# Layer 0's value and gate projections of a two-layer encoder: seven products of halves by Strassen's scheme in place of eight

## The chip, the cores and the metric

The kernel runs on one core of a Trainium2 chip. The metric is the time of one execution on the device, in microseconds (us). Engines are named as in the profile: PE is TensorE (PEld are its weight loads), DVE is VectorE, ACT is ScalarE, POOL is GpSimd, SP is SyncE, which starts most of the transfers.

## The reference

The input is x of 512 tokens by 1024 features. There are two layers, each with a normalisation that is modulated by a condition c, a mixer, and a gated residual. Layer 0's mixer is retention with 4 heads, layer 1's is forgetting attention. What matters here is the input of layer 0:

```python
shift, scale, gate = jnp.split(c_act @ mod_w[i] + mod_b[i], 3, axis=-1)
h = _rms_norm(x, norm_g[i]) * (1.0 + scale[:, None, :]) + shift[:, None, :]
...
q, k, v, g = jnp.split(h @ w_in, [RET_DK, 2 * RET_DK, 2 * RET_DK + RET_DV], axis=-1)
```

For each of the 4 heads, q and k have 256 columns of `w_in`, v and g have 512. So v and g of a head are two products of h (512 x 1024) with 1024 x 512 weights, eight such products in all. q and k get a rotation by position. v is later used with its mean over the 512 columns of a head taken off, g goes through SiLU. All is float32.

## The kernel before

Every float32 product is made of three matmuls in the type fp32r: an operand is split into a head (ACT casts it to fp32r: `wh` for weights, the first `act` for activations) and a rest (what is left, by a subtraction on DVE or, in a few places, on POOL: `wl` and the second `act`). The function `mm3` adds head x head, head x rest and rest x head in a PSUM bank.

The weights come in as blocks of 512 KB ([128, 1024] words, tile `raw`), in one list that sets their order (class `Stream`). The class `WItem` loads a block and splits it. Blocks of `mod_w` (class `MItem`) stream between them; their steps (tile `macc`, one operation of 512 words for 128 rows) make the modulation for layer 0 at the start, and later, spread over the heads of layer 0, gate of layer 0 and modulation of layer 1.

The start: x is normalised and transposed. `make_h` makes, for each of 8 groups of 128 features, the modulated activations h, transposed ([128 features, 512 tokens]), with ACT once as head and once in full, and the rest on DVE. As these come, q and k of head 0 and q of head 1 are projected in six PSUM banks (tile `s`). POOL and DVE make the table of cosine and sine (tiles `tg`, `trig`). Then `rope` rotates: four DVE products of 512 words per projection (`rt`), and two additions and two rests on POOL (`rt`, `act`).

Then come heads 0 to 3 (`head`): q and k by `proj_qk`, where the weights stand and h moves; v and g by `proj_b`, where a block of h stands (128 features by 128 tokens) and 512 columns of weights move: 4 token tiles x 8 feature blocks x 3 = 96 matmuls of 512 columns per projection, into four banks of kind `p`. `evac_v` copies a bank with its sum and makes head and rest of v less its mean, `evac_g` puts SiLU of a bank in the tile `big`. Beside the projections of head h runs the retention of head h - 1 (`merge` gives it 0.45 of the projections' TensorE time). After it come the output projection of layer 0 (tile `a`), the second normalisation, and layer 1.

The order of instructions on each engine is not the program's. The class `Sched` collects all instructions as tasks, plays them through a simple model of the engines, with a price for each (`cost`), a number of buffers for each kind of tile (`KINDS`) and a priority from the program's place, and emits them in the order in which that model starts them. So a changed price or pool moves instructions everywhere. Each engine then takes its instructions strictly in that order. All instructions have one line in the profile, that of the emitting call (L430), so groups are told apart by their tiles.

Of the kernel before, what the change touches and what calls it, by code (L numbers as in the profile page):

```python
# [43 lines left out]
KINDS = {  # L44
# [3 lines left out]
    "goh": ("C", 16), "wo": ("C", 16), "raw": ("B", N_B), "wh": ("W", 3), "wl": ("W", 3),  # L48
# [11 lines left out]
def host_constants():  # L60
# [6 lines left out]
    # sums over the tokens up to c: [m, c] for the diagonal block, ones after it  # L67
# [10 lines left out]
class View:  # L78
    """A part of a buffer that may have no address yet: slices are taken once the buffer has one.
    `part` and `idx` say which partitions and words it covers."""  # L80
# [21 lines left out]
    def rearrange(self, pattern, **sizes):  # L102
        """Of "p (a b) -> p a b" and "p a b -> p (a b)", the only forms in use."""
# [35 lines left out]
class Buf:  # L139
# [6 lines left out]
    def touch(self, task, view, write):  # L146
        """The earlier tasks that an access has to follow."""
# [20 lines left out]
class Sched:  # L168
    """Collects the instructions of the kernel with what they read and write, plays them through a
    simple model of the core (engines in order of their own, transfers, memory slots) and emits  # L170
# [61 lines left out]
    def cost(self, t, op, args, kw, ins, outs):  # L232
# [8 lines left out]
        if t.eng == "PE":  # L241
            if op == "transpose":
                t.cols = 256
                return 0.107
# [265 lines left out]
def trunk(tc, x, c, positions, mod_w, mod_b, norm_g, ret_w_in, ret_w_out, fox_w_in, fox_b_f,  # L510
# [6 lines left out]
    with ExitStack() as es:  # L517
# [280 lines left out]
        def W(key, i=0):  # L798
            it = st.need(where[key] + i)
            return it.h, it.l  # L800
# [693 lines left out]
```

## Time and profile before

| | before |
|---|---|
| time, median of 3 runs | 757.44 us (756.97 to 757.86) |
| span of the profiled execution | 757.8 us (the page gives no other time for it; the runs' times lie within 0.9 us of it) |
| granted TensorE clock, mean | 0.989 |
| bytes moved | 105.73 MB, mean 140 GB/s |
| instructions | 10002 |

How to read it: times are counted from the span's start. A group of instructions has its engine, operation, tiles (out<-in), shapes and number, and behind the bar the time in which one of them was busy, the mean duration of one in ns, and the idle time of the engine just before them with what ended it. For PE the moving operand stands first among the inputs, then the stationary one, so `p<-wh,act` is a matmul that moves weights past standing activations. A timeline's row has start and length of a run of like instructions. [...]

### The profile page before, as it was taken

What the parts mean: (1) busy time and instruction counts of PE and PEld (TensorE: products, weight loads), DVE (VectorE), ACT (ScalarE), POOL (GpSimd) and SP (SyncE); (2) the same over time, 40 slices, a digit from 0 to 9 for tenths busy, and PEclk for the clock granted to TensorE, in tenths of its full rate; (3) what the DMA queues carried; (4) which work ended last, traced back from release to release, by engine and by line L of the source; (5) the groups of instructions that cost most, each with busy time, mean ns of one, the idle gap of its engine ahead of it and who ended that gap; (6) DMA issues with size and microseconds to landing.
All of it is one profiled execution on the core that took longest, in us unless ns stands there. A gap on an engine that the chain in (4) does not pass through costs nothing.

```text
span 757.8 us, 10002 instructions
## 1 busy us (share of the span) xinstructions
PE 735.2 (97%) x3478; PEld 603.2 (80%) x3478; DVE 540.3 (71%) x1168; ACT 359.5 (47%) x688; POOL 160.6 (21%) x156
## 2 busy tenths in 40 slices
PE   8999999999999999999999999999999899999995
PEld 6777888888888888888888887678888788888884
DVE  5886745865585458757764477978798879889945
ACT  7433623244224332443323255438576567777723
POOL 3437800300330033000000100342133422221011
PEclk9899999999999999999999999999999999999999
DMA  8993251644255334504532513434334425658002
GB/s 285 349 328 122 64 195 56 192 156 140 83 167 161 131 112 132 187 30 131 175 116 96 219 56 128 150 135 108 117 96 135 133 53 133 160 137 301 0 1 111
DMA packets 69730, 105.73 MB, mean 140 GB/s; under 512 B 6200, under 2 KB 35120, under 8 KB 69680
## 3 DMA queue, kind: packets, MB, share of 16 engines
q1 hardware_dynamic: 66320, 98.78, 40.4%
q0 software_dynamic: 3360, 6.32, 3.5%
q8 instruction: 27, 0.44, 0.2%
q14 instruction: 23, 0.19, 0.1%
HBM read 96.64 MB, written 4.25 MB: 133 GB/s over the span
## 4 chain that ended last, share of the span: by engine, by line
PE 79%; DVE 7%; issue 1%; ACT 1%; DMA 1%; POOL 1%; SPq 0%; POOLq 0%; ACTq 0%; DVEq 0%
PE p L430 46%; PE a L430 17%; PE r L430 15%; DVE t L430 3%; DVE wl L430 1%; DVE lg L430 1%; DVE macc L430 1%; POOL qn L430 1%; DMA ck<-cum_dram 1%; ACT tm L430 0%; DVE z L430 0%; DVE ph L430 0%; ACT qn L430 0%; DMA cum_dram<-tm 0%; DVE x L430 0%
## 5 line engine op out<-in xcount | busy, mean ns | idle before, releaser
L430 DVE TENSOR_TENSOR wl<-raw,wh 128x1024 fp32r<-128x1024 f32 x92 | 119.2, 1296 | 81.7 <-ACT wh L430 76.1
L430 ACT CAST wh<-raw 128x1024 fp32r<-128x1024 f32 x96 | 100.4, 1049 | 155.9 <-PE p L430 94.3
L430 PE MATMUL p<-wh,act 128*128 128x512 f32 x512 | 161.3, 391 | 1.8 <-DVE rt L430 1.8
L430 PE MATMUL p<-wh,big 128*128 128x512 f32 x384 | 134.8, 404 | 0.0
L430 PEld LDWEIGHTS p<-wh,act 128*128 128x128 f32 x512 | 96.0, 188 | 22.0 <-DVE rt L430 2.2
L430 PE MATMUL p<-wl,act 128*128 128x512 f32 x256 | 99.8, 390 | 0.0
L430 PEld LDWEIGHTS p<-wh,big 128*128 128x128 f32 x384 | 71.9, 189 | 14.8
L430 DVE SCALAR_TENSOR_TENSOR macc<-raw,csilu,macc 128x512 f32<-128x512 f32 x82 | 77.2, 941 | 1.2
L430 PE MATMUL p<-wl,big 128*128 128x512 f32 x192 | 76.6, 399 | 0.0
L430 PE MATMUL a<-wh,act 128*128 128x512 f32 x192 | 62.4, 398 | 0.6 <-ACT act L430 0.6
L430 POOL TENSOR_TENSOR rt<-rt,rt 128x512 f32<-128x512 f32 x16 | 25.3, 1599 | 176.4 <-DVE rt L430 176.4
L430 PEld LDWEIGHTS p<-wl,act 128*128 128x128 f32 x256 | 48.1, 188 | 9.9
L430 PE MATMUL p<-act,wh 128*128 128x512 f32 x160 | 53.8, 394 | 0.0
L430 POOL TENSOR_TENSOR ck<-ck,mask 128x256 f32<-128x256 f32 x32 | 28.1, 898 | 118.3 <-DMA ck<-cum_dram 81.9
L430 PE MATMUL p<-big,wh 128*128 128x512 f32 x128 | 44.4, 411 | 0.0
L430 ACT ACTIVATE lg<-lg,t 128x128 f32<-128x128 f32 (+1 forms) x64 | 36.1, 565 | 15.9 <-DVE t L430 15.2
L430 PEld LDWEIGHTS a<-wh,act 128*128 128x128 f32 x192 | 36.0, 188 | 8.2 <-ACT act L430 0.8
L430 PEld LDWEIGHTS p<-wl,big 128*128 128x128 f32 x192 | 36.4, 189 | 5.9
L430 PE MATMUL r<-act,sh 128*128 128x512 f32 x120 | 40.0, 394 | 0.0
L430 PE MATMUL a<-wl,act 128*128 128x512 f32 x96 | 37.8, 394 | 0.0
L430 POOL DMA_DIRECT2D x_dram<-x x8 | 4.4, 552 | 144.1 <-DVE x L430 137.6
L430 PEld LDWEIGHTS p<-act,wh 128*128 128x128 f32 x160 | 30.0, 188 | 5.9
(167 smaller groups left out, 1421.5 us busy)
## 6 DMA issues: line engine op xcount, KB each, us to landing
raw<-in_ret_w_in SPq DMA_DIRECT2D x48, 512.0 KB, 4.6
raw<-in_mod_w SPq DMA_DIRECT2D x64, 256.0 KB, 5.0
raw<-in_fox_w_in SPq DMA_DIRECT2D x32, 512.0 KB, 5.3
raw<-in_mod_w SPq DMA_DIRECT2D x16, 512.0 KB, 3.9
raw<-in_ret_w_out SPq DMA_DIRECT2D x16, 512.0 KB, 4.7
ck<-cum_dram SPq DMA_DIRECT2D x16, 448.0 KB, 4.0
x<-in_x SPq DMA_DIRECT2D x16, 256.0 KB, 3.5
st<-st POOLq DMA_DIRECT2D x32, 128.0 KB, 2.8
```

Source lines behind the costliest of these rows:

```text
L430: getattr(eng, op)(*[real(v) for v in args], **{k: real(v) for k, v in kw.items()})
```

## The change

For v and g of each head, the 512 tokens, the 1024 features and the 512 columns are halved. With h in quarters (tokens i, features j) and the weights in quarters b11, b21, b12, b22 ([512 features, 256 columns], one block of 512 KB each), Winograd's form of Strassen's scheme gives the four quarters of the result by seven products of quarters, instead of eight, and sums before and after. A product of quarters is 2 token tiles x 4 feature blocks x 3 = 24 matmuls of 256 columns.

- `sums_of_h`: for each of four pairs of feature groups, four sums of activations (256 words each) on POOL (tiles `sx`), and two splits of 512 words (ACT and DVE, tiles `sf4`), kept for all heads.
- Each of the eight projections (`strassen`) forms four differences of weight blocks on DVE in place (tile `raw`, 1024 words each) and splits seven blocks rather than four. All the rests are now on DVE.
- A bank `p` holds both token tiles of a product. Three times in a projection ACT copies a bank aside (tile `u`), three quarters of the result are a bank plus such a copy, on DVE, and one is the bank itself. The last product accumulates in the bank that the quarter before it was read from.
- `put_v` adds the quarters of v with their sums, and makes head and rest as before (tile `vr2`). `put_g` adds the quarters of g on DVE, and ACT takes SiLU.
- Buffers: 56 instead of 48 of 512 words, and one pool of 16 of 1024 words, instead of 9 + 6 + 2, for incoming, split and a few other blocks (up to 10 incoming, 4 heads and 4 rests rather than 3 and 3). POOL's queue for transfers gets 4096 bytes per partition of room.
- The model's price of a matmul of m columns is 0.002 + m / 2260 us, at least 0.109, instead of m / 2400, at least 0.107.

```diff
-N_C, N_B = 48, 9
+N_C, N_B = 56, 16
...
-    "st": ("C", 12), "ck": ("K", 2), "lg": ("C", 6), "ph": ("C", 10), "v": ("C", 8), "oT": ("C", 8),
-    "goh": ("C", 16), "wo": ("C", 16), "raw": ("B", N_B), "wh": ("W", 3), "wl": ("W", 3),
+    "st": ("C", 12), "ck": ("B", 2), "lg": ("C", 6), "ph": ("C", 10), "v": ("C", 8), "oT": ("C", 8),
+    "goh": ("C", 16), "wo": ("C", 16), "raw": ("B", 10), "wh": ("B", 4), "wl": ("B", 4), "vr2": ("B", 2),
+    "sf4": ("C", 16), "sx": ("C", 4), "u": ("C", 4),
...
-            return max(0.107, m / 2400.0) if args[2].dtype == F32R else max(0.107, m / 600.0)
+            return max(0.109, 0.002 + m / 2260.0) if args[2].dtype == F32R else max(0.109, m / 600.0)
...
+        def w_s(src, col):
+            return [Block(src[:, 4 * i:4 * i + 4, col + 256 * j:col + 256 * j + 256])
+                    for i, j in ((0, 0), (1, 0), (0, 1), (1, 1))]
...
+        def sums_of_h(k):
+            lo, hi = hf32[k], hf32[k + 4]
+            a, b = slice(0, 256), slice(256, 512)
+            s13, s24 = s.buf("sx"), s.buf("sx")
+            with s.at(-4.0):
+                G.tensor_tensor(out=s13[:, a], in0=lo[:, b], in1=hi[:, b], op=ALU.add)
+                G.tensor_tensor(out=s13[:, b], in0=lo[:, a], in1=lo[:, b], op=ALU.subtract)
+                G.tensor_tensor(out=s24[:, a], in0=s13[:, a], in1=lo[:, a], op=ALU.subtract)
+                G.tensor_tensor(out=s24[:, b], in0=hi[:, a], in1=s24[:, a], op=ALU.subtract)
+                for src, (n1, n2) in ((s13, (1, 3)), (s24, (2, 4))):
+                    h, l = s.buf("sf4", 512, F32R), s.buf("sf4", 512, F32R)
+                    split(src, h, l)
+                    forms[n1][k] = (h[:, a], l[:, a])
+                    forms[n2][k] = (h[:, b], l[:, b])
...
+            def heads(src):
+                h, l = s.buf("wh", 1024, F32R), s.buf("wl", 1024, F32R)
+                split(src, h, l)
+                return [(h[:, k * 256:k * 256 + 256], l[:, k * 256:k * 256 + 256]) for k in range(4)]
+
+            def less(out, a, b):
+                V.tensor_tensor(out=out, in0=a, in1=b, op=ALU.subtract)
+                return heads(out)
+
+            def product(bank, a, w, new):
+                with s.at(PROC):
+                    w = w()
+                a = a()
+                for tl in range(2):
+                    ts = slice(tl * P, tl * P + P)
+                    for k in range(4):
+                        mm3(bank[:, tl * 256:tl * 256 + 256], a[k][0][:, ts], a[k][1][:, ts], *w[k],
+                            new and tl == 0 and k == 0, tl == 1 and k == 3, skip_group_check=True)
+                        yield 0.354
+
+            def keep(bank):
+                u = s.buf("u")
+                A.copy(u, bank)
+                return u
+
+            x = pt_()
+            yield from product(x, lambda: quarter(0, 0), lambda: heads(block(b11)), True)
+            u1 = keep(x)
+            y = pt_()
+            yield from product(y, lambda: quarter(0, 1), lambda: heads(block(b21)), True)
+            put(0, 0, y, u1)
+            v = pt_()
+            yield from product(v, lambda: forms[1], lambda: less(block(b11), block(b12), block(b11)), True)
+            u5 = keep(v)
+            yield from product(x, lambda: forms[2], lambda: less(block(b11), block(b22), block(b11)), False)
+            u2 = keep(x)
+            yield from product(v, lambda: forms[4], lambda: heads(block(b22)), False)
+            put(0, 1, v, u2)
+            yield from product(x, lambda: forms[3], lambda: less(block(b12), block(b22), block(b12)), False)
+            put(1, 1, x, u5)
+            yield from product(x, lambda: quarter(1, 1), lambda: less(block(b21), block(b21), block(b11)), False)
+            put(1, 0, x, None)
...
+                    if rest is None:
+                        A.activation(dst, bank[:, cs], AF.Identity, accum_out=sm)
+                    else:
+                        V.tensor_tensor_reduce(out=dst, in0=bank[:, cs], in1=rest[:, cs], scale=1.0,
+                                               scalar=0.0, op0=ALU.add, op1=ALU.add, accum_out=sm)
...
+                if rest is not None:
+                    V.tensor_tensor(out=dst, in0=src, in1=two(rest), op=ALU.add)
+                    src = dst
+                A.activation(dst, src, AF.Silu)
...
-            yield from proj_b(lambda i: W(("v", h), i), hT, evac_v(h))
-            yield from proj_b(lambda i: W(("g", h), i), hT, evac_g(h))
+            yield from strassen(("v", h), put_v(h))
+            yield from strassen(("g", h), put_g(h))
...
-    nc = bacc.Bacc("TRN2", target_bir_lowering=False, num_devices=1)
+    nc = bacc.Bacc("TRN2", target_bir_lowering=False, num_devices=1, dynamic_dma_scratch_size=4096)
```

The functions that make a product's operands are called where the product begins in the program; `PROC` moves the split of weights 6 us ahead in the priorities. `quarter(i, j)` are the splits of h that were there before; `forms[1]` to `forms[4]` are the sums of activations.

More of the change, by code (lines that the diff above doesn't have):

```diff
@@ L796, in trunk, with R @@
         st = Stream(s, items)
+        def R(key, i):
+            return st.need(where[key] + i).raw
         def W(key, i=0):
@@ L985, in evac_g, with two, strassen, block @@
-        def evac_g(h):
+        def two(v):
+            return v.rearrange("p (k n) -> p k n", k=2, n=256)
+        def strassen(key, put):
+            b11, b21, b12, b22 = range(4)
+            raw = {}
+            def block(i):
+                if i not in raw:
+                    raw[i] = R(key, i)
+                return raw[i]
+            def heads(src):
[36 more added lines that the diff above has]
+            put(1, 0, x, None)
@@ L986, in evac_g, with put_g, put @@
+        def put_g(h):
             gt = big(F32)
             go[h] = [gt[:, t, :] for t in range(NT)]
[L989 to L991 removed]
+            def put(i, j, bank, rest):
+                dst = gt[:, 2 * i:2 * i + 2, j * 256:j * 256 + 256]
+                src = two(bank)
+                if rest is not None:
+                    V.tensor_tensor(out=dst, in0=src, in1=two(rest), op=ALU.add)
+                    src = dst
+                A.activation(dst, src, AF.Silu)
+            return put
```

68 lines of the change are left out of this document (44 added, 24 removed), and 2 rows, old and new, of the table KINDS.

## The prediction

> **What bounds the kernel now.** I read the page first, then busy time by stage, then the groups by form, then timelines of single instructions.
>
> ```profile
> span 757.8 us, 10002 instructions
> PE 735.2 (97%) x3478; PEld 603.2 (80%) x3478; DVE 540.3 (71%) x1168; ACT 359.5 (47%) x688; POOL 160.6 (21%) x156
> PE 79%; DVE 7%; issue 1%; ACT 1%; DMA 1%; POOL 1%; SPq 0%; POOLq 0%; ACTq 0%; DVEq 0%
> ```
>
> TensorE is busy for 97% of the span and carries 79% of the chain that ended last. The span, 757.8 us, lies 0.4 us above the median of the timed runs (757.44), so nothing that counts lies around it; I add to 757.8. The change works in layer 0's four heads. Here are the stretches of heads 0, 1, 2 and 3 (columns: stretch, its length, busy time of PE, PEld, DVE, ACT and POOL, granted clock, DMA share, GB/s).
>
> ```profile
> 67.00:114.00 47.00, 45.25 (x199) 37.09 (x198) 28.76 (x35) 19.16 (x32) 21.61 (x14) 1.00 0.43 138
> 114.00:180.00 66.00, 66.00 (x298) 54.73 (x297) 41.89 (x80) 24.89 (x44) 6.93 (x4) 1.00 0.44 140
> 180.00:255.00 75.00, 75.00 (x342) 62.30 (x341) 46.72 (x86) 25.36 (x42) 12.95 (x8) 1.00 0.44 140
> 255.00:330.00 75.00, 75.00 (x347) 62.55 (x346) 48.70 (x94) 25.40 (x42) 12.98 (x8) 1.00 0.39 127
> sum 263.00, PE 261.25 PEld 216.66 DVE 166.07 ACT 94.82 POOL 54.47; mean PE 65.31 PEld 54.16 DVE 41.52 ACT 23.70 POOL 13.62
> ```
>
> TensorE fills 261 of these 263 us at full clock. VectorE works 166 of 263, so it has 97 us to spare. The question is whether the change asks for more than that.
>
> **TensorE: fewer columns, in shorter matmuls.** Value and gate have the weights moving and the activations standing:
>
> ```profile
> L430 PE MATMUL p<-wh,act 128*128 128x512 f32 x512 | 161.3, 391 | 1.8 <-DVE rt L430 1.8
> L430 PE MATMUL p<-wl,act 128*128 128x512 f32 x256 | 99.8, 390 | 0.0
> 139.76 0.62 PE L430 MATMUL p<-wh,act 128*128 128x512 f32 x2
> 149.28 0.62 PE L430 MATMUL p<-wh,act 128*128 128x512 f32 x2
> ```
>
> These are 768 matmuls of 512 columns. Between the two timeline rows lie 14 groups of three, so one takes (149.28 - 139.76) / 42 = 0.2267 us, start to start. After the change there are 8 projections x 7 products x 24 = 1344 matmuls of 256 columns. Retention has a few of that width:
>
> ```profile
> 117.35 0.28 PE L430 MATMUL r<-act,act 128*128 128x256 f32 x1
> 117.47 0.39 PE L430 MATMUL p<-act,wh 128*128 128x512 f32 x1
> 117.70 0.40 PE L430 MATMUL r<-act,act 128*128 128x256 f32 x2
> 117.93 0.39 PE L430 MATMUL p<-act,wl 128*128 128x512 f32 x1
> ```
>
> One takes 0.12 from its start to the next start, a pair 0.23. Half of the wide one, 0.1133, is the floor; 0.12 is the ceiling. I take 0.116, near the pair, which is what a long row of them looks most like. Removed: 768 x 0.2267 = 174.1. Added: 1344 x 0.116 = 155.9. TensorE saves 18.2 us (12.8 at 0.12, 21.8 at the floor). This is all that the change can win in layer 0.
>
> **VectorE: what it must do more.** Each projection now has seven blocks to split, not four, and four differences of weight blocks to form, all on VectorE in operations of 1024 words. Durations in a row overlap the next one's start, so I price by distance between starts.
>
> ```profile
> 258.62 1.23 DVE L430 TENSOR_TENSOR wl<-raw,wh 128x1024 fp32r<-128x1024 f32 x1 [1.05 <-ACT wh L430]
> 259.76 0.55 DVE L430 TENSOR_TENSOR sf<-r,dec 128x384 f32<-128x384 f32 x1
> 686.44 0.68 DVE L430 TENSOR_TENSOR raw<-raw,gate 128x512 f32<-128x512 f32 x1
> 687.04 0.68 DVE L430 CUSTOM_DVE_ANT_1 lg<-r,ck 128x512 f32<-128x512 f32 x1
> 690.49 0.42 DVE L430 CUSTOM_DVE_ANT_1 lg<-r,ck 128x256 f32<-128x256 f32 x1
> 690.95 0.70 DVE L430 TENSOR_TENSOR oT<-r,tm 64x512 f32<-64x512 f32 x1
> ```
>
> A rest of 1024 words costs 1.14, an operation of 512 words 0.60, an addition of 256 words with its sum 0.46. Added are: 24 rests x 1.14 = 27.4; 32 differences x 1.14 = 36.5 (no row shows one; size and operands are those of a rest); 24 additions with sums for the values x 0.46 = 11.0; 12 additions for the gates x 0.60 = 7.2; 8 rests of the sums of activations x 0.60 = 4.8. Together 86.9, of which nothing replaces older work. So 166.1 + 86.9 = 253.0, against a TensorE that would need 263 - 18.2 = 244.8.
>
> Some of it lies outside the stage. By the order below and the rows ahead of it, four of the small rests, the first block's rest and two differences come before the stage (2.4 + 1.1 + 2.3 = 5.8); and at the end of the stage VectorE has today already done some 5 us for the output projection (4 gate products and 2 rests), which it will then do later. That leaves 253.0 - 5.8 - 5.0 = 242.2.
>
> **The collision with GpSimd.** VectorE's operations on two SBUF tensors get slower while GpSimd works. First the groups in 67 to 330, then single rows of VectorE and GpSimd:
>
> ```profile
> L430 DVE TENSOR_TENSOR wl<-raw,wh 128x1024 fp32r<-128x1024 f32 x43 | 59.2, 1376 | 45.0 <-ACT wh L430 44.9
> L430 DVE SCALAR_TENSOR_TENSOR macc<-raw,csilu,macc 128x512 f32<-128x512 f32 x42 | 40.0, 952 | 0.6
> L430 DVE SCALAR_TENSOR_TENSOR act<-vr,t,act 128x512 fp32r<-128x512 f32 x16 | 13.0, 816 | 4.5 <-ACT act L430 4.2
> L430 DVE TENSOR_TENSOR wl<-raw,wh x11: 1224/1226/1227, 354.0 to 415.5; 128x1024 fp32r<-128x1024 f32 x11
> 231.31 0.74 DVE L430 SCALAR_TENSOR_TENSOR macc<-raw,csilu,macc 128x512 f32<-128x512 f32 x1
> 134.94 5.18 DVE L430 SCALAR_TENSOR_TENSOR macc<-raw,csilu,macc 128x512 f32<-128x512 f32 x3
> 132.64 3.52 POOL L430 TENSOR_TENSOR rt<-rt,rt 128x512 f32<-128x512 f32 x2 [40.99 <-DVE rt L430]
> 136.13 3.44 POOL L430 TENSOR_TENSOR act<-rt,act 128x512 fp32r<-128x512 f32 x2
> ```
>
> Without GpSimd a rest takes 1.226 and a step of the modulation 0.74; beside a rotation on GpSimd (132.64 to 139.6) a step takes 5.18 / 3 = 1.73, 0.98 more. Over the stage this costs 43 x 0.15 + 42 x 0.21 = 15.3 us today. It grows with the share of time in which VectorE runs such operations: now (59.2 + 40.0 + 13 for the values' rests) / 263 = 43%, then (112.2 + 27.4 + 36.5 + 4.8) / 263 = 69%: 15.3 x 69 / 43 = 24.6, so 9.3 more. GpSimd also gets 16 new additions of 256 words; at half of 0.98 each, 69% of the time, 5.4 more. VectorE's demand becomes 242.2 + 14.7 = 256.9, within bounds of 242.2 (no more collisions) and 266.2 (each of the 32 rotations' operations costs 0.98 and each sum 0.49: 39.2 instead of 15.3).
>
> [...]
>
> **What fills VectorE can't fill all of the time.** It is at its fullest in layer 1:
>
> ```profile
> 620.00:640.00 20.00, 20.00 (x112) 16.85 (x111) 18.59 (x46) 15.17 (x38) 5.92 (x8) 1.00 0.46 114
> 640.00:660.00 20.00, 20.00 (x114) 17.01 (x113) 16.71 (x44) 16.02 (x38) 5.79 (x8) 1.00 0.53 139
> 660.00:680.00 20.00, 19.93 (x112) 16.69 (x111) 17.75 (x45) 14.53 (x35) 5.04 (x8) 1.00 0.53 144
> 680.00:700.00 20.00, 20.00 (x113) 16.90 (x111) 19.91 (x53) 14.14 (x33) 2.33 (x2) 1.00 0.91 307
> 700.00:720.00 20.00, 20.00 (x92) 16.43 (x91) 19.73 (x32) 15.78 (x29) 0.00 (x0) 1.00 0.00 0
> ```
>
> The best two slices give 99%, all five 92.7 / 100 = 93%. I take the middle, 96%: heads 0 to 3 then take 256.9 / 0.96 = 267.6 us, 4.6 more than the 263 of now. TensorE waits for the difference, 267.6 - 244.8 = 23 us, in the products.
>
> Where that shows first is head 0. On VectorE, before the change, behind the first blocks of v (rt: rotation of q and k from PSUM, wl: rest of a weight block):
>
> ```order
> L430 TENSOR_TENSOR rt_731<-s_362,trig_649 128x512
> L430 TENSOR_TENSOR rt_746<-s_362,trig_704 128x512
> L430 TENSOR_TENSOR wl_755<-raw_543,wh_742 128x1024
> L430 TENSOR_TENSOR rt_764<-s_375,trig_704 128x512
> L430 TENSOR_TENSOR rt_770<-s_375,trig_649 128x512
> L430 TENSOR_TENSOR rt_781<-s_409,trig_649 128x512
> L430 TENSOR_TENSOR wl_793<-raw_597,wh_779 128x1024
> ```
>
> And now, at the same place (sf: rests of the sums of activations, raw: differences of weight blocks):
>
> ```order
> L431 TENSOR_TENSOR sf_151_731<-sx_575,sf_147_718 128x512
> L431 TENSOR_TENSOR wl_736<-raw_464,wh_726 128x1024
> L431 TENSOR_TENSOR wl_749<-raw_441,wh_739 128x1024
> L431 TENSOR_TENSOR raw_441<-raw_513,raw_441 128x1024
> L431 TENSOR_SCALAR tg_707<-tg_707 128x512
> L431 TENSOR_TENSOR sf_161_785<-sx_742,sf_159_772 128x512
> L431 TENSOR_TENSOR raw_464<-raw_464,raw_441 128x1024
> L431 TENSOR_TENSOR rt_802<-s_344,trig_796 128x512
> L431 TENSOR_TENSOR sf_168_808<-sx_769,sf_164_800 128x512
> ```
>
> Of these rows two in seven read two SBUF tensors before, now seven in nine, just where GpSimd is busiest (21.6 of 47 us).
>
> **The start.** On GpSimd the table of cosine and sine (tg) followed at once on the last rest of q and k:
>
> ```order
> L430 TENSOR_TENSOR wl_407<-raw_301,wh_397 128x1024
> L430 TENSOR_TENSOR wl_523<-raw_372,wh_510 128x1024
> L430 TENSOR_SCALAR tg_560<-tg_546 128x512
> L430 TENSOR_SCALAR tg_580<-tg_560 128x512
> L430 TENSOR_TENSOR tg_585<-tg_580,tg_546 128x512
> ```
>
> Now eight sums of activations (sx) stand ahead of it:
>
> ```order
> L431 TENSOR_TENSOR wl_503<-raw_357,wh_477 128x1024
> L431 TENSOR_TENSOR sx_371<-x_341,x_500 128x256
> L431 TENSOR_TENSOR sx_537<-sx_371,x_341 128x256
> L431 TENSOR_TENSOR sx_546<-x_351,x_510 128x256
> L431 TENSOR_TENSOR sx_537<-x_500,sx_537 128x256
> L431 TENSOR_TENSOR sx_546<-x_351 128x256
> L431 TENSOR_TENSOR sx_566<-sx_546,x_351 128x256
> L431 TENSOR_TENSOR sx_575<-x_437 128x256
> L431 TENSOR_TENSOR sx_566<-x_510,sx_566 128x256
> L431 TENSOR_SCALAR tg_595<-tg_579 128x512
> ```
>
> The nearest row is GpSimd's addition of 256 words to the mask:
>
> ```profile
> L430 POOL TENSOR_TENSOR ck<-ck,mask 128x256 f32<-128x256 f32 x32 | 28.1, 898 | 118.3 <-DMA ck<-cum_dram 81.9 <-DVE t L430 30.3 <-DVE lg L430 6.1
> ```
>
> Eight of them are 7 us by which the table, and the rotations behind it, come later. The first product (24 x 0.116 = 2.8 us) fills part of that on TensorE. I add 1 us (0 to 4).
>
> **What costs nothing, and its cover.** ScalarE gets 24 more casts of weight blocks and 24 copies of a bank:
>
> ```profile
> L430 ACT CAST wh<-raw 128x1024 fp32r<-128x1024 f32 x96 | 100.4, 1049 | 155.9 <-PE p L430 94.3 <-PE a L430 16.1 <-issue 12.4
> L430 ACT ACTIVATE big<-p 128x512 f32<-128x512 f32 x16 | 9.5, 596 | 8.1 <-PE p L430 8.1
> ```
>
> That is 24 x (1.05 + 0.60) = 40 us on 95 of 263; it stays half idle. The transfers carry the same bytes; 32 blocks come in rows half as long, with a DMA share of 0.44 at most. In each projection the seventh product accumulates in a bank that VectorE must first have read (a wait behind whatever VectorE has queued; behind it on TensorE stand its 24 matmuls and the next projection); the order puts other products or retention between, and if that cover is gone the wait is part of the 23 us. Layer 1 is the same code in a new order; I take 0 (-3 to +3).
>
> Sum: 757.8 + 4.6 + 1.0 = 763.4, rounded to **763**. With 99% instead of 96% it is 755, with 93% 772.
>
> **The rivals.** First, and on the other side: *VectorE keeps up.* The larger pools (4 instead of 3 pairs of split blocks, more room for raw ones) let it work ahead while q and k are projected, where it has time, so that TensorE never waits. For it: with no more collisions the demand is 242.2, just under the 244.8 of TensorE. Against it: 99% for 240 us was only seen over 40. Time: 757.8 - 18.2 = 740 (736 to 745). It decides if TensorE's idle time in heads 0 to 3 stays under 10 us. Chance 0.25. Second: *every collision is paid in full*: 266.2 / 0.96 = 277.3, 14.3 more than 263, 773 with the start; up to 782 if stalls of over 2 us also lower the granted clock. Chance 0.15. The forecast has 0.60. That the saving of columns doesn't come through (0.1295 per matmul would cancel it) is excluded by the 0.12 row.
>
> **How the numbers follow.** About 0.2% (1.5 us) can be told from no change. The forecast runs from 755 to 772: slower 0.48, the same 0.07, faster 0.05. With the first rival's 0.25 faster is 0.30; with the second's 0.15 slower is 0.63; same is 0.07. The range leaves out the lower half of the first rival and the upper part of the second: 742 to 779.
>
> **What would show it.** Right: VectorE at 95% or more from 67 us to head 3's gate, rests of weights at a mean over 1.376, TensorE idle or waiting for wl some 23 us there, and matmuls of 256 columns 0.113 to 0.12 apart. Wrong: TensorE without gaps there (first rival), or matmuls further apart than 0.12, or gaps that wait for something other than VectorE.

## The result, and the profile after

| | before | after |
|---|---|---|
| time, median | 757.65 us (756.97 to 759.26, 4 runs) | 769.87 us (767.45 to 770.64, 4 runs) |
| ratio | | 1.0153, 95% interval 1.0133 to 1.0174 |
| span of the profiled execution | 757.8 us | 765.7 us |
| granted TensorE clock in it | 0.989 | 0.985 |

The change makes the kernel slower, by 11.6 us (10.1 to 13.2). The forecast was 763, some 5.5 us slower. The profiled execution is the least of the four (767.45 us, a span of 765.7 and 1.75 outside it); in the others the granted clock was 0.978 to 0.980 and the time 769.8 to 770.6. The spans differ by 7.9 us, so the traces show 8 of the 12 us between the medians. The other 4 stand in no trace of this pair; a clock lower by 0.006 over 768 us would be some 4.6 us of TensorE's time, by estimate.

The first lines of the page after, to set beside those of before:

```profile
span 765.7 us, 11375 instructions
PE 725.9 (95%) x4050; PEld 618.2 (81%) x4050; DVE 631.1 (82%) x1292; ACT 391.0 (51%) x728; POOL 185.0 (24%) x172
```

TensorE has 9.3 us less to do and is late all the same. Where, the stretches tell (columns as in the prediction; the first is the end of the start, then come the four of heads 0 to 3):

```profile
40.00:67.00 27.00, 20.18 (x101) 15.79 (x100) 25.38 (x30) 11.25 (x15) 20.50 (x15) 1.00 0.62 198
67.00:114.00 47.00, 35.64 (x223) 31.41 (x221) 41.40 (x50) 20.89 (x31) 42.21 (x28) 0.93 0.26 77
114.00:180.00 66.00, 65.31 (x473) 61.60 (x474) 64.06 (x116) 34.67 (x57) 6.81 (x4) 1.00 0.38 125
180.00:255.00 75.00, 74.08 (x497) 68.11 (x496) 68.82 (x120) 34.44 (x55) 14.95 (x8) 1.00 0.44 137
255.00:330.00 75.00, 74.58 (x503) 68.61 (x502) 67.28 (x119) 34.09 (x53) 14.95 (x8) 1.00 0.48 151
```

And the first of them before:

```profile
40.00:67.00 27.00, 25.49 (x111) 20.25 (x110) 18.59 (x28) 12.02 (x15) 16.54 (x14) 0.94 0.69 231
```

From 114 to 330 us TensorE is busy for 65.31 + 74.08 + 74.58 = 214.0 of 216 us, with VectorE at 200.2 of 216 (93%): the heads that the forecast saw starving are full. From 40 to 114 us it is busy for 55.8 of 74 (before: 70.7). There VectorE went from 47.4 to 66.8 us and GpSimd from 38.2 to 62.7. The loss is all in the start and head 0. Head 0's last gate matmul, after and then before:

```profile
134.49 0.28 PE L431 MATMUL p<-wh,act 128*128 128x256 f32 x1
```

```profile
113.78 0.39 PE L430 MATMUL p<-wh,act 128*128 128x512 f32 x1
```

It starts 20.7 us later, of which 5 are other matmuls (the start of head 0's retention, and six matmuls of q or k) that now stand ahead of it. From there to head 3's last gate matmul (rows further below) it is 208.6 us instead of 220.2. These 5 us are missing there, and 2 us of the output projection have come in. Like for like, start and head 0 cost some 15.7 us, and heads 1 to 3 give back some 8.7. What TensorE waited for between 40 and 135 us, after (the five largest of nine) and then before:

```profile
PE p L431 <- ACT wh L431: 7.0, 2, 4.9
PE s L431 <- DVE wl L431: 4.5, 2, 3.2
PE p L431 <- DVE rt L431: 1.5, 1, 1.5
PE p L431 <- DVE wl L431: 1.1, 2, 0.7
PE r L431 <- POOL act L431: 0.9, 1, 0.9
```

```profile
PE p L430 <- DVE rt L430: 1.8, 1, 1.8
PE r L430 <- DVE macc L430: 0.7, 1, 0.7
PE s L430 <- DVE wl L430: 0.7, 1, 0.7
```

The longest wait, 4.9 us, is before the third product, the first one that needs sums of activations. Rows of TensorE's timeline there, and 5 us on:

```profile
78.83 0.28 PE L431 MATMUL p<-wh,act 128*128 128x256 f32 x1
83.98 0.58 PE L431 MATMUL p<-wh,sf 128*128 128x256 f32 x1 [4.87 <-ACT wh L431]
86.08 0.58 PE L431 MATMUL p<-wh,sf 128*128 128x256 f32 x1 [1.51 <-DVE rt L431]
86.45 0.41 PE L431 MATMUL p<-wl,sf 128*128 128x256 f32 x1
87.09 0.41 PE L431 MATMUL p<-wl,sf 128*128 128x256 f32 x1
...
91.24 0.40 PE L431 MATMUL p<-wh,sf 128*128 128x256 f32 x2
96.58 0.40 PE L431 MATMUL p<-wh,sf 128*128 128x256 f32 x2
```

ScalarE and GpSimd at that time, and GpSimd's end of the table before:

```profile
82.36 0.62 ACT L431 CAST sf<-sx 128x512 fp32r<-128x512 f32 x1 [5.89 <-POOL sx L431]
82.89 1.04 ACT L431 CAST wh<-raw 128x1024 fp32r<-128x1024 f32 x1
83.84 0.63 ACT L431 ACTIVATE trig<-tg 128x512 f32<-128x512 f32 x1
```

```profile
78.73 1.70 POOL L431 TENSOR_TENSOR sx<-sx,x 128x256 f32<-128x256 f32 x1
80.39 1.26 POOL L431 TENSOR_TENSOR tg<-tg,tg 128x512 f32<-128x512 f32 x1
81.61 0.72 POOL L431 TENSOR_TENSOR sx<-x,sx 128x256 f32<-128x256 f32 x1
```

```profile
65.87 4.43 POOL L430 TENSOR_TENSOR tg<-tg,tg 128x512 f32<-128x512 f32 x2
```

The cast of the weights (`wh`, 82.89) stands on ScalarE behind a cast of sums (`sf`), that one waits 5.89 us for GpSimd, and GpSimd's sums (`sx`) stand between the steps of the table (`tg`). GpSimd is done with the table at 80.39 + 1.26 = 81.65 us; before it was at 65.87 + 4.43 = 70.3. The rotations follow on it. Who waited for the sums, by the view of that tile:

```profile
who waited for it (us, times):
  ACT sf L431: 13.4, 5
```

So a queue of small additions on GpSimd reaches TensorE through ScalarE's queue, which the forecast had as half idle.

Behind the wait stands a second price: from 86.45 to 87.09 us three matmuls take 0.64 us, from 91.24 to 96.58 us fifteen threes take 5.34, 0.356 each. The first stand under a halved clock. In stretches of 5 us, from 80 us on:

```profile
80.00:85.00 5.00, 0.58 (x1) 0.29 (x1) 2.92 (x3) 2.64 (x5) 5.00 (x6) 0.90 0.48 157
85.00:90.00 5.00, 3.92 (x18) 3.93 (x19) 4.32 (x7) 3.69 (x5) 3.61 (x4) 0.50 0.00 0
90.00:95.00 5.00, 5.00 (x41) 5.00 (x40) 5.00 (x10) 3.03 (x5) 5.00 (x3) 0.92 0.02 5
```

That is 2 x (0.10 + 0.50 + 0.08) x 5 = 6.8 us at half clock. For the first 2 of them, up to 86.08, TensorE has nothing to do but one matmul; the 22 matmuls behind lose 0.213 - 0.119 each, 2.1 us. Nor is all of it new: before, the 0.94 in the stretch from 40 to 67 us is 0.06 x 2 x 27 = 3.2 us at half clock. That the wait lowers the clock is read from their order alone. In the trace of before, too, 2.02 us without a matmul, up to 603.38 us, are followed by a clock of 0.50 from 604 to 606 us. What sets it off no run tested.

### The profile page after: what moved, and what is told of

It reads as the page before. It is cut to its first block, busy times and chain, and to the rows that moved or that the text cites. A ratio compares the mean times of both kernels' runs of the same rounds, so it can differ in the third digit from the quotient of the medians.

```text
span 765.7 us, 11375 instructions
## 1 busy us (share of the span) xinstructions
PE 725.9 (95%) x4050; PEld 618.2 (81%) x4050; DVE 631.1 (82%) x1292; ACT 391.0 (51%) x728; POOL 185.0 (24%) x172
## 5 line engine op out<-in xcount | busy, mean ns | idle before, releaser
L431 DVE TENSOR_TENSOR wl<-raw,wh 128x1024 fp32r<-128x1024 f32 x116 | 153.8, 1332 | 8.6 <-ACT wh L431 5.1
L431 ACT CAST wh<-raw 128x1024 fp32r<-128x1024 f32 x120 | 125.0, 1048 | 66.2 <-PE p L431 27.6
L431 PE MATMUL p<-wh,sf 128*128 128x256 f32 x512 | 96.6, 287 | 8.5 <-ACT wh L431 7.0
L431 PEld LDWEIGHTS p<-wh,sf 128*128 128x128 f32 x512 | 81.6, 193 | 9.6 <-ACT wh L431 7.5
L431 PE MATMUL p<-wh,act 128*128 128x256 f32 x384 | 72.5, 282 | 2.7 <-DVE t L431 2.7
L431 PE MATMUL p<-wl,sf 128*128 128x256 f32 x256 | 73.2, 286 | 0.0
L431 PEld LDWEIGHTS p<-wh,act 128*128 128x128 f32 x384 | 60.6, 188 | 4.3 <-DVE t L431 3.5
L431 PE MATMUL p<-wl,act 128*128 128x256 f32 x192 | 54.3, 283 | 1.4 <-DVE wl L431 1.1
L431 PEld LDWEIGHTS p<-wl,sf 128*128 128x128 f32 x256 | 49.3, 192 | 0.1
L431 DVE TENSOR_TENSOR raw<-raw,raw 128x1024 f32<-128x1024 f32 x32 | 45.4, 1419 | 0.2
L431 ACT ACTIVATE lg<-lg,t 128x128 f32<-128x128 f32 (+1 forms) x64 | 36.1, 565 | 15.7 <-DVE t L431 15.1
```

Source lines behind the costliest of these rows:

```text
L431: getattr(eng, op)(*[real(v) for v in args], **{k: real(v) for k, v in kw.items()})
```

## The experiments

Two theories at first. **Start:** the loss sits ahead of 115 us. **Forecast:** VectorE is too full in all four heads, and each loses. Each group of kernels ran on one chip beside the kernel before (medians of it 758.1 to 759.4 us); ratios are to that. Where times of two changed kernels are subtracted, they can come from different chips, and 1 us is not to be relied on.

| kernel | median, us | ratio, 95% interval |
|---|---|---|
| pools and price only | 763.98 | 1.0081, 1.0051 to 1.0112 |
| head 0 only | 779.15 | 1.0276, 1.0244 to 1.0308 |
| heads 1 to 3 only | 760.30 | 1.0029, 1.0010 to 1.0047 |
| sums on VectorE | 768.98 | 1.0146, 1.0116 to 1.0175 |
| before, 64 bytes on | 759.26 | 0.9996, 0.9978 to 1.0015 |
| after, 64 bytes on | 769.31 | 1.0126, 1.0103 to 1.0150 |
| after, 32 bytes on | 769.39 | 1.0124, 1.0099 to 1.0149 |
| heads 1 to 3 only, 64 bytes on | 761.09 | 1.0034, 1.0014 to 1.0054 |
| before, split weights low | 764.48 | 1.0078, 1.0049 to 1.0107 |
| after, weights high | 768.95 | 1.0130, 1.0102 to 1.0159 |
| heads 1 to 3 only, weights high | 760.38 | 1.0019, 1.0001 to 1.0038 |
| after, sums cut | 762.85 | 1.0045, 1.0023 to 1.0068 |
| after, head 0's differences cut | 763.40 | 1.0064, 1.0038 to 1.0089 |
| after, differences of heads 1 to 3 cut | 766.48 | 1.0112, 1.0084 to 1.0141 |
| after, all differences and sums cut | 755.13 | 0.9947, 0.9929 to 0.9966 |
| after, sums after the table | 772.52 | 1.0188, 1.0153 to 1.0223 |
| heads 1 to 3 only, sums later | 764.30 | 1.0070, 1.0044 to 1.0095 |
| heads 1 to 3 only, sums on VectorE | 760.55 | 1.0024, 1.0004 to 1.0043 |

### Which part, in which head

In the second and third of these kernels both forms of the projections stand, and the head decides:

```diff
+            if h in SEVEN:
                 yield from strassen(("v", h), put_v(h))
                 yield from strassen(("g", h), put_g(h))
+            else:
+                yield from proj_b(lambda i: W(("v", h), i), hT, evac_v(h))
+                yield from proj_b(lambda i: W(("g", h), i), hT, evac_g(h))
```

*Pools and price only* (in the kernel before, the change's `KINDS`, `N_C`, `N_B`, `cost` and scratch size; `KINDS` also has 36 instead of 40 buffers for `act`).

> The kernel before with nothing of Strassen's scheme, only with the change's pools (56 and 16 buffers, 10 incoming, 4 + 4 split blocks), its price of a matmul and its 4096 bytes for GpSimd's queue. Both theories (start: the loss sits ahead of 115 us, where sums of activations hold up GpSimd and VectorE; full VectorE: each of the four heads loses) say that these are worth nothing by themselves: 757.5, within 1.5 us. A third theory, that the new pools and prices reorder the start or layer 1 for the worse, says 760 or more.

*Head 0 only.*

> Only head 0 by seven products, heads 1 to 3 as before; sums of activations as in the change. Start theory: all of the loss and none of the gain that lies in heads 1 to 3 (there the two profiles differ by 208.6 - 220.3 = -11.6 us), so 769.9 + 11.6 = 781, 777 to 784. Full VectorE: a quarter of the loss, 757.5 + 12.3 / 4 = 760.6, at most 765.

*Heads 1 to 3 only.*

> Head 0 as before, heads 1 to 3 by seven products, and the 16 sums of activations on GpSimd only after the last rotation of the start (58 and 15 buffers, since the order doesn't close with 56 and 16). Start theory: the gain of heads 1 to 3 alone, 757.5 - 11.6 = 746, 743 to 750. Full VectorE: three quarters of the loss, 757.5 + 9.2 = 766.7, at least 760.

This one has the sums after the last rotation (`turned`), in a new place:

```diff
-            if kt >= 4:
-                sums_of_h(kt - 4)
...
         run(head(0))
+        with s.after(turned):
+            for k in range(4):
+                sums_of_h(k)
```

*Sums on VectorE* (`V.tensor_tensor` for `G.tensor_tensor` in the four lines of `sums_of_h`).

> The change with its 16 sums of activations on VectorE instead of GpSimd, all else as it is. Start theory: GpSimd's table and rotations aren't held up by 16 additions of 1.2 us any more, VectorE pays 16 x 0.34 = 5.4 us for them and is rid of collisions; a good half of the start's loss of 20 us goes, 758, 755 to 763. Full VectorE: 5.4 us more for VectorE, 775, at least 770.

Measured 764.0, 779.2, 760.3 and 769.0. Head 0 costs 779.2 - 764.0 = 15.2 us: the forecast's theory, at most 765 for that kernel, has fallen. But the start theory missed too. Heads 1 to 3 only took 760.3 where it said 746, and the forecast's theory at least 760. The pools and the price alone cost 6 us, which neither theory had. And the sums cost as much on VectorE as on GpSimd (the 0.34 us each of the expectation is an estimate, the price in the kernel's `cost`: 0.069 + 256 / 960). Nor do the parts add: head 0 costs 15.2 beside the old form, 769.9 - 760.3 = 9.6 beside the new one, as heads 1 to 3 only has the sums, too, to pay for in head 0. The stretch of head 0 with the sums on VectorE:

```profile
67.00:114.00 47.00, 39.03 (x225) 35.03 (x225) 44.04 (x63) 20.18 (x29) 29.29 (x18) 0.84 0.25 77
```

GpSimd is down from 42.2 to 29.3 us, VectorE up from 41.4 to 44.0 of 47, and the granted clock is down to 0.84. VectorE is at 94%, so work taken from GpSimd to it finds little room; and the clock is at half for some 15 us (0.16 x 2 x 47) where it was for 6.8. Which of the two takes the gain was not separated.

### The six microseconds of the pools

The seven kernels that follow move all buffers by a few bytes (four of them, by `const("pad", [16])` or `[8]` ahead of the buffers) or choose where a pool lies (three), and change no instruction. In `emit`, for the latter:

```diff
             self.sent = self.order()
+            for ph, lo, hi, n in [('W', 0, 6, 1024)]:
+                for i in range(lo, hi):
+                    self.phys[ph][1].tile([P, n], F32, tag=f"{ph}{i}", bufs=1, name=f"place_{ph}{i}")
```

*Before, 64 bytes on.*

> The kernel before, with 64 unused bytes ahead of all its buffers, and the same instructions in the same order. Of its 68 large buffers 43 began at 32 and 24 at 96 past a multiple of 128 bytes; now it is the other way round, as in the kernel with only the pools and the price (which took 764.0, and whose wide matmuls stand 231 ns apart in the value and gate projections, where they stood 227 in the kernel before). Place theory: matmuls whose operands begin at 96 take 3 to 4 ns longer, so about 2000 x 3.8 = 7.6 us: 764, 761 to 766, with the projections' matmuls at 230 ns or more. Order theory (the pools' other order costs the 6 us, and the pitch has another cause): 758, within 1.5 us, matmuls 227 apart.

*After, 64 bytes on.*

> The changed kernel with 64 unused bytes ahead of all its buffers, so that 71 large ones begin at 32 instead of 96 past a multiple of 128 bytes. Place theory: some 1500 wide matmuls are 3.8 ns shorter, 5.7 us, and the 1344 narrow ones perhaps 2 ns, 2.7 us: 769.9 - 7 = 763, 760 to 766. Order theory: 769.9, within 1.5.

*After, 32 bytes on.*

> The changed kernel with 32 unused bytes ahead, so that 72 large buffers begin at a multiple of 128 bytes. Place theory doesn't say whether 0 is as good as 32 or better; if a multiple of 128 is what counts, it is at least as good: 763 or less. Order theory: 769.9, within 1.5.

*Heads 1 to 3 only, 64 bytes on.*

> Head 0 as before, heads 1 to 3 by seven products, sums of activations after the last rotation, as in the run that took 760.3, with 64 unused bytes ahead (72 large buffers at 32 instead of 96). Place theory: some 2000 wide matmuls 3.8 ns shorter: 760.3 - 7 = 753, 751 to 756, under the kernel before. Order theory: 760.3, within 1.5.

All four: no difference. The offset within 128 bytes is not it. What was left of the theory is the region:

*Before, split weights low.*

> The kernel before with its six buffers for split weights at the lowest addresses (25184 to 49760 bytes) instead of 114848 to 153760, same instructions in the same order. In the kernel with only the pools and the price the value and gate matmuls stand 226.7 ns apart where both parts of a weight block lie over 106000, 229 where only the rest lies under 70300, 233 to 234.5 where the head does. Place theory (the moving operand's place in SBUF sets the pitch): 768 x 6.6 ns = 5.1 us more in layer 0 alone, 762 at least, and a pitch of 233. Order theory (the pools cost 6 us by the order that they make): the time of the kernel before, within 1.5 us, pitch 227.

*After, weights high* (the four buffers of `big` and 30 of 512 words first, then the pool of weights).

> The changed kernel with the same instructions in the same order, its 16 buffers for weights at 107104 to 172640 bytes instead of 11 of them at 29280 to 74336. Place theory: most of the 6 us by which the pools and the price alone are slower come back, 764, 762 to 766. Order theory: the time of the changed kernel, 769.5, within 1.5.

*Heads 1 to 3 only, weights high.*

> The run with head 0 as before and heads 1 to 3 by seven products (760.3), its 15 buffers for weights at 107104 bytes and over. Place theory for the wide matmuls alone: 192 of head 0, some 290 of the output projection, 240 of q and k and 140 of the start get 2 to 4 ns back, 2.5 us: 758. If place is worth nothing here, as it was for the whole change: 760.5.

The kernel before takes 5.1 us more with its six split blocks at the low end (764.48 against 759.37), with the same instructions. Its value and gate matmuls in a row:

```profile
141.09 0.63 PE L433 MATMUL p<-wh,act 128*128 128x512 f32 x2
151.58 0.63 PE L433 MATMUL p<-wh,act 128*128 128x512 f32 x2
```

Fifteen threes lie between: (151.58 - 141.09) / 45 = 0.2331 us each, where the rows of the prediction give 0.2267; 768 x 6.4 ns = 4.9 us. So the place of the buffers is worth 5 us there, and the new single pool put most of the weights low. In the kernel with pools and price only, whose weights lie partly high, those matmuls stand 0.2311 apart in the mean: 768 x 4.2 ns = 3.2 of its 6 us, and the rest has no shown cause. The changed kernel wins nothing from high weights (768.95 against 769.3 to 769.9), nor does heads 1 to 3 only (760.38 against 760.30): their value and gate matmuls are 256 wide, but for head 0 of the latter, and in rows without a gap those of the change are 0.119 apart in the mean, with low weights. The place explains half of the loss by the pools alone, and none of the change's loss.

### What head 0 waits for

In the next four kernels instructions stay in their order, but some are cut to 16 words, with the model's price left as it was. The edit of the second of them:

```diff
-                V.tensor_tensor(out=out, in0=a, in1=b, op=ALU.subtract)
+                n = 16 if key[1] == 0 else 1024
+                t = V.tensor_tensor(out=out[:, 0:n], in0=a[:, 0:n], in1=b[:, 0:n], op=ALU.subtract)
+                t.cost = 0.069 + 1024 / 960.0
                 return heads(out)
```

*After, sums cut* (the four lines of `sums_of_h` on 16 words, the splits behind them on activations).

> The changed kernel with its 16 sums of activations on GpSimd cut to 16 words each, priced in the model as before, so that the order stays (the splits read activations instead of sums, so the output isn't the reference's). Sums theory (the 16 additions of 1.2 us hold up the table and slow VectorE, and that is head 0's loss): 10 to 15 us less, 755 to 760. Local theory (in head 0 VectorE has more to do than TensorE, as it had no retention of an earlier head beside it): only the collisions go, some 3 us, 765 to 768.

*After, head 0's differences cut.*

> The changed kernel with the 8 differences of weight blocks of head 0 cut to 16 words each, same order (the output isn't the reference's). They take 8 x 1.42 = 11 us of VectorE. Local theory: TensorE follows VectorE there, 6 to 11 us less, 759 to 764. Sums theory: VectorE isn't what is waited for, 2 us less at most, 768 or more.

*After, differences of heads 1 to 3 cut.*

> The changed kernel with the 24 differences of weight blocks of heads 1 to 3 cut to 16 words, same order, head 0 whole (the output isn't the reference's). 24 x 1.4 = 34 us less for VectorE. Local theory (heads 1 to 3 already have TensorE without gaps; only head 0 waits for VectorE): 3 us less at most, 766 to 769.5. Forecast's theory (VectorE is full in all four heads and sets their length): 8 us less or more, 761 or under.

*After, all differences and sums cut.*

> The changed kernel with all 32 differences and the 16 sums cut to 16 words, same order but for a few rows (the output isn't the reference's). Sums alone gave 769.5 - 762.9 = 6.6 us, head 0's differences alone 6.1. If both stand one behind the other on VectorE's path in head 0, they add: 769.5 - 12.7 = 757, and up to 3 less from heads 1 to 3: 753 to 758. If they are two views of one wait: 761 to 763.

Measured 762.9, 763.4, 766.5 and 755.1. The first lies between the two theories: the sums cost more than their collisions and less than all of head 0's loss. The others are as the local theory says. A difference takes 1.42 us in the changed kernel:

```profile
L431 DVE TENSOR_TENSOR raw<-raw,raw 128x1024 f32<-128x1024 f32 x32 | 45.4, 1419 | 0.2
```

So cutting 8 x 1.42 = 11 us of VectorE's work in head 0 gives 6.1 us; cutting 24 x 1.42 = 34 us of the same work in heads 1 to 3 gives 3.0. And all together give 769.5 - 755.1 = 14.4, about the sum of the parts (6.6 + 6.1 + 3.0 = 15.7; 769.5 stands for the changed kernel's three medians of 769.3 to 769.9). The traces say the same by place. Head 0's last gate matmul starts at 134.5 us in the change, at 128.7 with the sums cut, 129.7 with head 0's differences cut and 123.9 with all cut; from there to head 3's last it is 208.6, 208.8, 208.6 and 206.6 us. So in head 0 VectorE and GpSimd stand one behind the other on the path to TensorE, and in the other heads they hardly do. But with all of them cut head 0 still ends 10 us later than before (5 of these are the matmuls that now stand ahead), and the kernel is only 0.5% faster than before: the sums and differences are about two thirds of the loss in start and head 0, and the rest was not taken apart. The stretches of heads 1 to 3 with their differences cut:

```profile
114.00:180.00 66.00, 65.50 (x477) 61.70 (x476) 57.28 (x119) 34.80 (x59) 6.81 (x4) 1.00 0.37 119
180.00:255.00 75.00, 75.00 (x507) 69.25 (x506) 61.04 (x122) 35.28 (x55) 13.00 (x8) 1.00 0.45 143
255.00:330.00 75.00, 75.00 (x508) 69.24 (x508) 57.92 (x119) 34.48 (x54) 13.05 (x8) 1.00 0.49 157
```

TensorE is busy for 215.5 of 216 us, where it was for 214.0: VectorE's 34 us were hidden but for some two. The cost in head 0 is local. The likely reason, which no run tested by itself: it has no retention of an earlier head to put beside the products, so what VectorE and GpSimd owe the products is owed at once.

### Where else the sums could go

```diff
             if kt >= 4:
-                sums_of_h(kt - 4)
+                with s.after(*table):
+                    sums_of_h(kt - 4)
```

*After, sums after the table* (`table` is the table's last step on GpSimd).

> The changed kernel with its 16 sums on GpSimd held back until the table of cosine and sine is done. If what the sums cost is the table that they hold up (its second half came 13 us later than before): most of their 6.6 us come back, 763 to 765. If it is GpSimd's time and the collisions in head 0 as such, whichever stands first: 768 or more, since then the third product waits for its sums instead.

*Heads 1 to 3 only, sums later* (`turned` is then one of the last activations of head 0's gate).

> Head 0 as before, heads 1 to 3 by seven products, and the 16 sums on GpSimd not at 90 to 110 us, beside head 0's splits, but from head 0's gate on, where GpSimd has nothing to do until 138 us. Local theory: head 0 ended 3.6 us later than before with the sums beside it (117.8 against 114.2 us); some 2 of that go, 758. If heads 1 to 3 are short of VectorE as well, the sums only collide there: 760 or more.

*Heads 1 to 3 only, sums on VectorE.*

> The same with the 16 sums on VectorE (0.34 us each, 5.4 in all) right after the last rotation of the start, so that GpSimd is out of it. Local theory: VectorE had 27% idle in head 0, which takes them; no collisions: 758. If not: 760 or more.

Measured 772.5, 764.3 and 760.6. With the table first, TensorE waits for the sums instead (from 40 to 140 us):

```profile
PE p L431 <- ACT sf L431: 6.4, 4, 3.0
PE p L431 <- DVE rt L431: 3.6, 1, 3.6
PE p L431 <- DVE sf L431: 2.8, 4, 1.1
```

And the clock is at half for longer, 0.22 x 2 x 47 = 21 us in the stretch of head 0:

```profile
67.00:114.00 47.00, 31.01 (x184) 26.54 (x182) 39.81 (x47) 19.85 (x30) 42.62 (x32) 0.78 0.30 87
```

So the table alone is not what the sums cost; head 0 needs both early, and whichever comes second is waited for. Moving the sums behind head 0's gate moved a loss into head 1: its value projection ran from 135.1 to 164.6 us, and from 135.4 to 160.2 with the sums earlier. TensorE waits 3.4 us there for a copy of a bank (`u`) that ScalarE makes late, and the granted clock from 114 to 180 us is 0.95; that the sums are behind this wait is not shown. Neither variant of heads 1 to 3 only reached the 758 of the local theory. No kernel with the whole scheme, and none with it in heads 1 to 3 alone, beat the kernel before; the nearest, heads 1 to 3 only, is 1.0019 to 1.0034 times as long in its four layouts and variants. In its profile the last gate projection ends 1.0 us later than before (335.4 against 334.4): head 0, with the sums beside it, ends 3.6 us later, and heads 1 to 3 give back 2.6. Their value and gate matmuls take 122.3 us of TensorE instead of 131.4 (by the distances between their starts), but TensorE waits 3.9 us for these:

```profile
PE p L432 <- ACT u L432: 2.4, 3, 0.8
PE p L432 <- DVE t L432: 1.5, 2, 1.2
```

Some 2 of the rest are two matmuls and twelve transposes of the output projection that now come earlier, and so no loss. Whether a better plan of the sums would bring this version under the kernel before was not settled.

## Why the prediction was right or wrong

The direction was right, and 769.9 lies in the range, but the move is twice the forecast's, and it comes from another place than the sum says: from the start and head 0, with heads 1 to 3 gaining. That the sum comes as near as it does is partly luck. Counting each matmul to the next one's start, or to its own end before a gap, TensorE's value and gate matmuls take 164.7 us instead of 175.3, all others 560.7 instead of 559.5, and the gaps 30.5 instead of 12.8: -10.6 + 1.2 + 17.7 = 8.3, for spans 7.9 apart. The forecast had -18.2 for the first and 24 for the last: 8 us too much saved, 6 us too much waited.

- **The base.** I took 757.8, the span, for the execution's whole time. In the runs the time is the span and 1.75 us more (767.45 for 765.7), so the profiled execution of before took some 759.5, 2 us above its median, and the forecast's move was rather 5.6 us on 757.4. This changes no term.
- **TensorE's saving.** Forecast 18.2 (12.8 to 21.8) with 0.116 per matmul. Measured (96.58 - 91.24) / 45 = 0.1187, so 174.1 - 1344 x 0.1187 = 14.6 at full clock. Nearer to the single row of 0.12 than to the pair that I chose: mis-sized by 3.6, within its bounds. Of the 14.6 only 10.6 are left in the trace: 2.1 go to the half clock, and the rest lies in head 0 too, where it was not taken apart. That the saving isn't cancelled was right.
- **VectorE's demand.** Forecast 242.2 without new collisions, 256.9 with. Measured from 67 to 330 us: 41.40 + 64.06 + 68.82 + 67.28 = 241.6, and 6.8 more before 67 us, where I had 5.8. But 330 us is no longer the end of head 3: up to its last gate matmul, at 343.4 us, VectorE is busy for 254.8, of which some 4 are already for the output projection. So the demand was about 250, between the two. The count of operations was right: over the whole span VectorE has 631.1 - 540.3 = 90.8 more, for 86.9 of work. The collisions were mis-sized. Rests, differences and steps of the modulation lose some 21 us to longer durations from 67 to 330 us; that is 6 more than the 15.3 of before, where I had 14.7 more, and 4 of the 6 fall in the 47 us of head 0. The rests there, and in heads 1 to 3 (1.22 at 114.78 us, where GpSimd is idle):

```profile
L431 DVE TENSOR_TENSOR wl<-raw,wh 128x1024 fp32r<-128x1024 f32 x8 | 13.6, 1714 | 0.0
L431 DVE TENSOR_TENSOR wl<-raw,wh 128x1024 fp32r<-128x1024 f32 x54 | 72.5, 1350 | 1.0 <-PE p L431 0.8
```

I scaled collisions with VectorE's share of exposed time over the whole stage, but GpSimd works for 42 of the 47 us of head 0's stretch and for 7 to 15 in a stretch after that. The upper bound of 266.2, each collision in full, did not hold: six of head 0's eight rests took 1.6 to 2.4 us beside GpSimd, but two, at 89.66 and 91.99 us, took 1.21 with GpSimd at work for 1.05 us and for all of it.

- **The fill of 96% over all four heads.** This step failed: "heads 0 to 3 then take 256.9 / 0.96", and TensorE waits for the difference, 23 us, in the products. I set one demand against one length for four heads, which lets head 0 borrow from the slack of the others, although I had written that the wait shows first in head 0. It can't borrow: from 40 to 114 us VectorE was at 66.8 of 74, and TensorE lost 70.7 - 55.8 = 14.9 us there; from 114 to 330 us VectorE ran at 93% with TensorE idle for 2.0 us. So in heads 1 to 3 TensorE set the length, and they gained; start and head 0 lost 15 to 16. The runs show it: the differences are worth 6.1 us in head 0 and 3.0 in the three others together.
- **The start.** "I add 1 us (0 to 4)" is the term that was farthest off. I priced eight sums on GpSimd and looked at the table alone. Of the 16, nine stand ahead of the table, two between its steps and five right behind it, ahead of the rotations. The table is 11 us late; ScalarE's queue hands the delay on to the weights; and behind the wait of 4.9 us the clock is at half, for 2.1 us of TensorE. Start and head 0 together cost 15.2 us (779.15 - 763.98).
- **The pools.** The forecast gave the new pools no price, and the first rival even counted on them. By themselves, with the price of matmuls, they cost 6.1 us (ratio 1.0081). The place of the weights accounts for 3.2 of these by the pace of that kernel's value and gate matmuls; in the changed kernel, with its narrow matmuls, high weights win nothing, so the place is no term of the change's sum. What the new pools and the price cost the changed kernel by its order no run shows.
- **The first rival** (VectorE keeps up) was right for heads 1 to 3: their value and gate matmuls take 120.8 us instead of 131.4 in the trace, TensorE is idle for 1.9, and between head 0 alone and all heads lie 779.15 - 769.87 = 9.3 us. By its own test, under 10 us of idle time in all four heads, it fell: from 67 us to head 3's last gate matmul TensorE is idle for 276.4 - 263.0 = 13.4. **The second** (each collision paid in full) was wrong in its mechanism: collisions took some 21 us where it had 39.2. Its 9 us for a lower clock stand on no row, and no run shows 2 us as a limit; the 6.8 us at half clock, behind the wait of 4.87 us, cost 2.1.
- **What was to show it.** VectorE at 95% or more up to head 3's gate: no, 254.8 of 276.4 us, 92%. TensorE idle or waiting for rests some 23 us: no, idle for 13.4, and by far not all of it for rests. Rests at a mean over 1.376: yes, if little:

```profile
L431 DVE TENSOR_TENSOR wl<-raw,wh 128x1024 fp32r<-128x1024 f32 x62 | 86.2, 1397 | 1.0 <-PE p L431 0.8
```

Matmuls 0.113 to 0.12 apart: yes. Gaps that wait for something other than VectorE: yes, the largest (7.0 us in two, for ScalarE, the longer one behind GpSimd), which I had named as a sign of being wrong.

- **Layer 1.** Forecast 0 (-3 to 3). The last gate matmul ends at 334.4 before and 343.4 after (rows below), so the rest takes 757.8 - 334.4 = 423.4 and 765.7 - 343.4 = 422.3; with the 2 us of output projection that now come earlier it is 1 us longer. Within the bounds.

```profile
334.02 0.40 PE L430 MATMUL p<-wh,act 128*128 128x512 f32 x1
```

```profile
343.13 0.28 PE L431 MATMUL p<-wh,act 128*128 128x256 f32 x1
```

## What to carry to other kernels

Set an engine's demand against the time stretch by stretch, not over a stage: here 11 us of differences on VectorE cost 6.1 us in head 0 and 34 us of them 3.0 in heads 1 to 3, and the slack that came later was no help to head 0. Price new small operations by what stands behind them in every queue that they or their consumers enter, since an engine that is half idle can still hand a wait on: ScalarE, busy for 20.9 of 47 us, waited 5.89 us for GpSimd, and TensorE 4.87 behind it. When pools are merged or resized, measure that alone first; it moves buffers, and with them the pace of instructions that nobody touched (here 0.2267 to 0.2331 us for a matmul of 512 columns).

## What the hardware showed that was not expected

- The place of the buffers changes the pace of this kernel's 512-column matmuls: 0.2267 us apart with the moving weights at 114848 bytes and over, 0.2331 with the same instructions and the weights at 25184 to 49760. A shift of all buffers by 64 bytes does nothing (759.26 us, a ratio of 0.9996). The kernel with 256-column matmuls, 0.119 apart in the mean, takes 768.95 us with high weights and 769.3 to 769.9 with low ones. Which property of the place it is (the weights' region, their distance from the other operand, or that other buffers move as well) was not separated.
- In these rows GpSimd is slowed as well, not only VectorE. An addition of 256 words on GpSimd took 1.70 us at 78.73 us, beside a difference of 1024 words on VectorE, and 0.72 at 81.61, beside an operation with one tensor as input. VectorE's rows at that time (an operation of the second kind takes 0.42 us at 59.79 us, where GpSimd is idle):

```profile
77.65 2.20 DVE L431 TENSOR_TENSOR raw<-raw,raw 128x1024 f32<-128x1024 f32 x1
81.68 0.93 DVE L431 TENSOR_SCALAR tg<-tg 128x512 f32<-128x512 f32 x1 [1.83 <-POOL tg L431]
```
